# Two gated FFN input projections as seven products per pair of tiles, on two token blocks of 428

## Chip, cores and metric

The kernel runs on one core of one Trainium2 chip. The metric is the device time of one execution in microseconds: 2782.41 us is the median of three runs (2781.95 to 2783.56).

## The reference, cut to what matters

A two-layer encoder trunk works on 1024 prompt tokens and 64 sample tokens that share all weights. Each layer is a mixer with residual, then a gated FFN with residual:

```
def conv_ffn(h, st, w_in, conv_w, conv_b, w_out):
    gu = h @ w_in                              # (1088 x 1024) @ (1024 x 5632)
    g, u = gu[..., :D_FF], gu[..., D_FF:]      # D_FF = 2816
    g, new_st = causal_dwconv(g, conv_w, conv_b, st)     # width 3, along the tokens
    return (gelu(g) * u) @ w_out, new_st       # back to 1024
...
x = x + mixer(rmsnorm(x, norm_mix[l]))         # layer 0: SSD + short conv; layer 1: RG-LRU
x = x + conv_ffn(rmsnorm(x, norm_ffn[l]), ...)
```

All of it is float32, and a last RMSNorm gives the output.

## The kernel before

Activations lie channel by token: a tile has 128 channels on the partitions and T = 1092 columns (1024 prompt tokens, 4 of padding, 64 sample tokens). A projection to one output tile of 128 channels takes KT = 8 input tiles. For accuracy each float32 operand is held as a rounded high part and a low part (the rest), both in the type `float32r`, and a product is three: high by high, low weight by high, high weight by low. The 1092 columns go through TensorE in NB = 3 blocks of BL = 364, each into its own bank of a PSUM tile `pm` (two of these tiles, three banks each). So one output tile costs 8 x 3 x 3 = 72 matmuls of 364 columns (`product`, L160, called by `project`, L176).

Weights come by the SP queue in float32 (`weights`, L122): two halves of 512 columns, each loaded into `raw`, copied to the high part `wh` on ACT (L131), and the low part `wl` subtracted on DVE (L132). `prefetch` (L173) does so ahead of a named projection.

The FFN (`ffn`, L603) handles its 22 tiles of the hidden width one at a time in `make` (L608): project the gate tile, multiply by the row scale of the RMSNorm RS (L615, out of PSUM), convolve (`conv`, L230: first tap on ACT, L236, two more on DVE, L238; history columns by POOL, L228), gelu on ACT (L618), times RS (L619), project the up tile, multiply it in (L622), and split the result into high and low `ring` tiles (L186, L187). `chunks` (L288) collects two such tiles and flushes them (`chunk`, L257): for each of the 8 output tiles, 18 matmuls over the two hidden tiles, and a DVE addition into the residual tile XR[m] (L262), which stays in SBUF (`xr`). At the last flush `Next` (L266) makes each finished XR[m] ready for the next stage: scaled and split into `xg` (L192, L193), squared on ACT (L282), and the squares summed by accumulating DMAs on POOL's queue (L283); with a spill, XR[m] is also written to DRAM (L275). `rms` (L204) turns the sums into RS. `finish` (L735) does the last flush of layer 1 block by block.

The code gives an order, but the order on each engine is set when the program is built, by a planner with modelled durations: of the instructions that are ready at a time it takes the one that stands first in the code. Buffers of a tag (`wk` has 5, `ring` 8, `xr` 8, `xg` 16, `raw` 3, `wh` and `wl` 6 each) are handed out as they come free, and the instruction that first writes one waits for that. Heads of the SSD advance in steps between matmuls (`between`, `tick`, L151).

```
for (wh, wl), (xh, xl) in terms:
    for w, x in ((wh, xh), (wl, xh), (wh, xl)):
        for b in range(NB):
            TE.matmul(ps[:, b, 0:BL], w, x[:, b * BL:(b + 1) * BL], start=i == 0, stop=i == n - 1)
```

Of the kernel before, what the change touches and what calls it, by code (L numbers as in the profile page):

```python
# [22 lines left out]
BL = T // NB  # L23
NCH = L // P
# [29 lines left out]
def program(nc, tc, a, ctx):  # L54
# [11 lines left out]
    def slot(tag, bufs, dt=F, cols=T):  # L66
        n_of[tag] = n_of.get(tag, 0) + 1
        return sl.tile([P, cols], dt, tag=tag, bufs=bufs, name=f"{tag}{n_of[tag]}")

    def xg(dt=R):  # L70
        return slot("xg", 16, dt)

    def xr(dt=F, cols=T):
        return slot("xr", 8, dt, cols)
# [47 lines left out]
    def weights(src):  # L122

        out = []
        for i in range(2):
# [3 lines left out]
            l = wp.tile([P, 512], R, tag="wl", bufs=6, name=f"wl{n}")  # L129
            nc.sync.dma_start(raw, src[:, i * 512:(i + 1) * 512])  # L130
# [59 lines left out]
    def split_scaled(src, scale, make):  # L190
        h, l = make(R), make(R)
# [4 lines left out]
    def sum_square(ss, src, first, by=V):  # L196
        if first:
            S.activation(ss, src, AF.Square)
        else:
            sq = wk()  # L200
            S.activation(sq, src, AF.Square)
            by.tensor_add(ss, ss, sq)

    def rms(ss, width, more=None):  # L204

        v, r, out = wk(), wk(), ss
# [49 lines left out]

    def chunk(xs, ws, XR, done=None):  # L257

        for m in range(KT):
            ps = psum()  # L260
            product(ps, [(piece(w, m), x) for w, x in zip(ws, xs)])
            V.tensor_add(b3(XR[m]), b3(XR[m]), ps[:, :, 0:BL])  # L262
            if done:
                done(m)

    class Next:  # L266


        def __init__(self, XR, key, make=None, spill=None):
            self.XR, self.key, self.xs, self.spill = XR, key, [], spill  # L270

        def __call__(self, m):
            self.xs.append(split_scaled(self.XR[m], col(self.key, m), xg))
            if self.spill is not None:
                nc.gpsimd.dma_start(self.spill[m], self.XR[m])  # L275
            if m == 0:
                self.ss = [slot("ss", 2), slot("ss", 2)]
            if m < 2:
                S.activation(self.ss[m], self.XR[m], AF.Square)
            else:  # L280
                sq = wk()
                S.activation(sq, self.XR[m], AF.Square)  # L282
                nc.gpsimd.dma_start(self.ss[m % 2], sq, accum_op=OP.add)  # L283
# [4 lines left out]
    def chunks(n, produce, w_out, XR, done, after):  # L288

        tiles = {}  # L290

        def flush(i):
            ws = [weights(w_out[i]), weights(w_out[i + 1])]
            if i + 2 == n and after:
                prefetch(after)
            use = [tiles.pop(i), tiles.pop(i + 1)]
            if i + 2 == n and not after:
                done(use, ws)
            else:
                chunk(use, ws, XR, done if i + 2 == n else None)  # L300

        for i in range(n):
            tiles[i] = produce(i)
            if i % 2 == 0 and 2 <= i < n - 2:
                flush(i - 2)
        flush(n - 4)
        flush(n - 2)
# [4 lines left out]
    for k in range(KT):  # L312
# [3 lines left out]
        XGs.append(split_scaled(t, col("mix0", k), xg))  # L316
        if k == 0:

            raw_dt = wp.tile([P, 512], F, tag="raw", bufs=3, name="raw_dt")[:, 0:3 * H * KT].rearrange("p (k n) -> p k n", k=KT)
            w_dt = wp.tile([P, 512], R, tag="wh", bufs=6, name="w_dt")[:, 0:3 * H * KT].rearrange("p (k n) -> p k n", k=KT)  # L320
# [115 lines left out]
    def heads(i, xs, zz):  # L436
# [64 lines left out]
        Hn = small([P, P], "hn", 1)  # L501
# [83 lines left out]
    XR, RS2 = [], {}  # L585
    for m in range(KT):
        t = xr()
        nc.gpsimd.dma_start(t, a["x"][:, m])
        XR.append(t)

    def ab_tile(i):
# [9 lines left out]
        return split(y, ring)  # L601

    def ffn(layer, XGs, rs, XR, done, after):  # L603
        kind = f"ffn{layer}"

        state = {}

        def make(f):  # L608
            ps = project(("f_in", layer, 2 * f), XGs)
            if f == 0:  # L610
                prefetch(("f_in", layer, 1))
                state["rs"] = rs()
            RS = state["rs"]
            cb = conv_buffer()
            V.tensor_mul(b3(cb[:, PAD:]), ps, b3(RS))  # L615
            g = wk()
            conv(cb, kind, f, g)
            S.activation(g, g, AF.Gelu_apprx_tanh)  # L618
            V.tensor_mul(g, g, RS)  # L619
            ps = project(("f_in", layer, 2 * f + 1), XGs)  # L620
            hh = wk()
            V.tensor_mul(b3(hh), ps, b3(g))  # L622
            return split(hh, ring)

        chunks(FT, make, a["f_out"][layer], XR, done, after)

    nxt = Next(XR, "fn0")
    chunks(16, ab_tile, a["ab_out"], XR, nxt, ("f_in", 0, 0))
    x_d = scratch("x_d", [KT, P, T])
    last, nxt = nxt, Next(XR, "mix1", spill=x_d)  # L630
    ffn(0, last.xs, last.rs, XR, nxt, ("lru_in", 8))
# [89 lines left out]
    XR = []  # L721
    for m in range(KT):
        t = xr()
        nc.gpsimd.dma_start(t, x_d[m])
        XR.append(t)

    def c_tile(i):
        g = wk()
        nc.gpsimd.dma_start(g, hs_d[i])
        return split(g, ring)  # L730

    nxt = Next(XR, "fn1")
# [183 lines left out]
```

## Time and profile before

| | |
|---|---|
| median of three runs | 2782.41 us |
| profiled execution | 2783.79 us |
| its span, first to last instruction | 2782.0 us |
| mean granted TensorE clock | 0.996 of 2.4 GHz |
| busy: PE, DVE, ACT, POOL | 99%, 56%, 29%, 7% |
| instructions: PE, DVE, ACT, POOL | 16660, 1723, 1083, 521 |

PE is TensorE's matmuls, PEld its weight loads, which run beside them. DVE is VectorE, ACT ScalarE, POOL GpSimd, SP the queue that issues most loads. A group's row gives line, engine, operation, out<-in, shape and count, then busy time and the mean duration of one in ns. Matmuls overlap in the records: the time that one takes from the next is read from the starts in a timeline, not from its duration.

### The profile page before, as it was taken

What the parts mean: (1) busy time and instruction counts of PE and PEld (TensorE: products, weight loads), DVE (VectorE), ACT (ScalarE), POOL (GpSimd) and SP (SyncE); (2) the same over time, 40 slices, a digit from 0 to 9 for tenths busy, and PEclk for the clock granted to TensorE, in tenths of its full rate; (3) what the DMA queues carried; (4) which work ended last, traced back from release to release, by engine and by line L of the source; (5) the groups of instructions that cost most, each with busy time, mean ns of one, the idle gap of its engine ahead of it and who ended that gap; (6) DMA issues with size and microseconds to landing.
All of it is one profiled execution on the core that took longest, in us unless ns stands there. A gap on an engine that the chain in (4) does not pass through costs nothing.

```text
span 2782.0 us, 39199 instructions
## 1 busy us (share of the span) xinstructions
PE 2747.3 (99%) x16660; PEld 2716.6 (98%) x16660; DVE 1569.0 (56%) x1723; ACT 803.4 (29%) x1083; POOL 195.4 (7%) x521
## 2 busy tenths in 40 slices
PE   8999999999999999999999999999999999999998
PEld 8999999999999999999999989999999999999997
DVE  7655665568665444444444567786644444444446
ACT  7323322232142112211211245551421211212223
POOL 1101111110000000000000010120000000000003
PEclk9999999999999999999999999999999999999999
DMA  3222322243231111111111141151311111111111
GB/s 132 78 82 82 100 98 82 83 132 135 71 94 40 44 46 46 46 43 46 42 46 46 63 131 58 55 196 57 89 44 46 45 44 46 42 46 44 41 47 68
DMA packets 85695, 193.08 MB, mean 69 GB/s; under 512 B 10096, under 2 KB 12704, under 8 KB 85520
## 3 DMA queue, kind: packets, MB, share of 16 engines
q1 hardware_dynamic: 67248, 123.40, 13.3%
q0 software_dynamic: 17984, 66.76, 8.0%
q8 instruction: 131, 2.15, 0.3%
q10 hardware_dynamic: 288, 0.42, 0.0%
q14 instruction: 44, 0.36, 0.0%
HBM read 156.81 MB, written 23.66 MB: 65 GB/s over the span
## 4 chain that ended last, share of the span: by engine, by line
PE 93%; DVE 2%; DMA 2%; issue 1%; ACT 1%; POOL 0%; DVEq 0%; POOLq 0%; ACTq 0%
PE pm L167 90%; DMA ss<-wk 2%; PE pa L514 1%; PE pa L487 1%; PE pm L750 1%; DVE xg L779 0%; PE pa L525 0%; PE pm L334 0%; DVE xr L262 0%; DMA hs_d<-ring 0%; PE pa L210 0%; PE pa L212 0%; PE pa L472 0%; DVE xg L193 0%; DMA par<-par 0%
## 5 line engine op out<-in xcount | busy, mean ns | idle before, releaser
L167 PE MATMUL pm<-xg,wh 128*128 128x364 f32 x7104 | 1409.1, 331 | 0.0
L167 PEld LDWEIGHTS pm<-xg,wh 128*128 128x128 f32 x7104 | 1205.2, 189 | 6.6 <-issue 3.1
L167 PE MATMUL pm<-xg,wl 128*128 128x364 f32 x3552 | 783.4, 329 | 0.0
L131 ACT ACTIVATE wh<-raw 128x512 fp32r<-128x512 f32 x440 | 274.4, 628 | 1472.6 <-PE pm L167 1250.8
L167 PE MATMUL pm<-ring,wh 128*128 128x364 f32 x3360 | 656.8, 329 | 5.7 <-DVE xr L262 1.9
L167 PEld LDWEIGHTS pm<-xg,wl 128*128 128x128 f32 x3552 | 620.6, 188 | 0.5
L167 PEld LDWEIGHTS pm<-ring,wh 128*128 128x128 f32 x3360 | 570.6, 188 | 8.3 <-DVE xr L262 2.5
L262 DVE TENSOR_TENSOR xr<-xr,pm 128x1092 f32<-128x1092 f32 x264 | 340.8, 1291 | 211.8 <-PE pm L167 205.8
L132 DVE TENSOR_TENSOR wl<-raw,wh 128x512 fp32r<-128x512 f32 x440 | 300.5, 685 | 252.5 <-ACT wh L131 252.2
L167 PE MATMUL pm<-ring,wl 128*128 128x364 f32 x1680 | 372.0, 330 | 0.0
L167 PEld LDWEIGHTS pm<-ring,wl 128*128 128x128 f32 x1680 | 293.5, 188 | 0.1
L238 DVE SCALAR_TENSOR_TENSOR wk<-wk,par,wk 128x1092 f32<-128x1092 f32 x104 | 140.9, 1355 | 64.1 <-ACT wk L236 62.6
L615 DVE TENSOR_TENSOR wk<-pm,ss 128x1092 f32<-128x1092 f32 x44 | 57.0, 1296 | 192.9 <-PE pm L167 192.7
L228 POOL COPY wk<-par 128x2 f32<-128x2 f32 (+1 forms) x72 | 40.5, 563 | 1723.7 <-DVE wk L615 1426.5
L622 DVE TENSOR_TENSOR wk<-pm,wk 128x1092 f32<-128x1092 f32 x44 | 57.0, 1295 | 119.6 <-PE pm L167 119.6
L187 DVE TENSOR_TENSOR ring<-wk,ring 128x1092 fp32r<-128x1092 f32 x68 | 88.0, 1296 | 38.6 <-ACT ring L186 32.8
L186 ACT ACTIVATE ring<-wk 128x1092 fp32r<-128x1092 f32 x68 | 75.7, 1116 | 101.5 <-PE pm L167 67.5
L236 ACT ACTIVATE wk<-wk,par 128x1092 f32<-128x1092 f32 x52 | 67.7, 1302 | 67.6 <-POOL wk L228 67.6
L619 DVE TENSOR_TENSOR wk<-wk,ss 128x1092 f32<-128x1092 f32 x44 | 57.0, 1297 | 52.1 <-ACT wk L618 52.1
L618 ACT ACTIVATE wk<-wk 128x1092 f32<-128x1092 f32 x44 | 49.2, 1118 | 120.8 <-DVE wk L238 120.8
L238 DVE SCALAR_TENSOR_TENSOR xr<-wk,par,xr 128x1092 f32<-128x1092 f32 x36 | 48.8, 1354 | 15.4 <-ACT xr L236 14.8
L193 DVE SCALAR_TENSOR_TENSOR xg<-xr,par,xg 128x1092 fp32r<-128x1092 f32 x32 | 43.3, 1354 | 10.7 <-ACT xg L192 10.4
(243 smaller groups left out, 1308.9 us busy)
## 6 DMA issues: line engine op xcount, KB each, us to landing
raw<-f_in SPq DMA_DIRECT2D x176, 256.0 KB, 2.5
raw<-ab_in SPq DMA_DIRECT2D x88, 256.0 KB, 2.6
raw<-f_out SPq DMA_DIRECT2D x88, 256.0 KB, 2.5
ss<-wk POOLq DMA_DIRECT2D x18, 546.0 KB, 7.0
ring<-at_d POOLq DMA_DIRECT2D x16, 546.0 KB, 6.1
raw<-ab_out SPq DMA_DIRECT2D x32, 256.0 KB, 2.6
raw<-lru_in SPq DMA_DIRECT2D x32, 256.0 KB, 2.5
xr<-x SPq DMA_DIRECT2D x8, 546.0 KB, 7.9
```

The lines of the kernel that those rows point to most:

```text
L131: S.activation(h, raw, AF.Copy)
L132: V.tensor_sub(l, raw, h.bitcast(F))
L167: TE.matmul(ps[:, b, 0:BL], w, x[:, b * BL:(b + 1) * BL], start=i == 0, stop=i == n - 1)
L186: S.activation(h, src, AF.Copy)
L187: V.tensor_sub(l, src, h.bitcast(F))
L236: S.activation(out, cb[:, at:at + T], AF.Identity, bias=col(kind + "_b", i), scale=col(kind + "_w", i * w))
L238: V.scalar_tensor_tensor(out, cb[:, at + k:at + k + T], col(kind + "_w", i * w + k), out, op0=OP.mult, op1=OP.add)
L262: V.tensor_add(b3(XR[m]), b3(XR[m]), ps[:, :, 0:BL])
L615: V.tensor_mul(b3(cb[:, PAD:]), ps, b3(RS))
L618: S.activation(g, g, AF.Gelu_apprx_tanh)
L619: V.tensor_mul(g, g, RS)
L622: V.tensor_mul(b3(hh), ps, b3(g))
```

## The change

In both FFNs, tiles are taken in pairs: two neighbouring gate tiles (or two up tiles) by the two halves of the 1024 inputs (HK = 4 tiles each) by two token blocks of SB = 428 columns are a two-by-two block product, computed with seven block products in place of eight (Winograd's form of Strassen's scheme). The sums of input blocks t1 to t4 are made once per layer (`Pairs`, a `Next`), the sums of weights for each pair of tiles (`Ready`), both ahead of the split into high and low parts. The last RB = 236 columns are projected plainly. `seven` issues the products in an order, copies partial sums that are used twice out of PSUM (`held`, on ACT) and goes on accumulating onto them; `Ready.step` is called four times in between for the next pair. All 22 pairs of a layer (11 gate, 11 up, in turn) come first; the gated rows go to DRAM (`h_d`) and are read back tile by tile for the output projection, which is done after them; the residual is written to DRAM and read back into `ring` tiles. Output weights are prepared for half the output tiles at a time, and the last chunks ahead of each FFN take four tiles at once. `wh`/`wl` have 4 buffers, `raw` 2 of twice the size; tags are x0, x1 (8 each), x2 (8 of 1284 columns) in place of xg and xr.

```diff
+SB = 428
+RB = T - 2 * SB
...
-            raw = wp.tile([P, 512], F, tag="raw", bufs=3, name=f"raw{n}")
-            h = wp.tile([P, 512], R, tag="wh", bufs=6, name=f"wh{n}")
+            raw = raws[:, i * 512:(i + 1) * 512]
+            h = wp.tile([P, 512], R, tag="wh", bufs=4, name=f"wh{n}")
...
+    PLACE = {"b21": (0, B[0]), "b22": (0, B[1]), "k1": (0, B[2]), "t3": (1, B[0]), "t4": (1, B[1]), "k0": (1, B[2]),
+             "t1": (2, B[0]), "t2": (2, B[1]), "b11": (2, slice(2 * SB, 3 * SB))}
+    class Pairs(Next):
+        order = [m for k in range(HK) for m in (k, k + HK)]
+        def operands(self, m):
+            if m < HK:
+                return
...
+            h, l = zip(*[(x(R), x(R)) for x in (x0, x1, lambda dt: x2(dt, 3 * SB))])
...
+            scaled(0, slice(0, T), r1, w1, slice(0, T))
+            S.activation(t4, r0[:, B[0]], AF.Copy, scale=w0)
+            V.scalar_tensor_tensor(t1, r0[:, B[1]], w0, t4, op0=OP.mult, op1=OP.subtract)
+            V.scalar_tensor_tensor(t2, r1[:, B[1]], w1, t1, op0=OP.mult, op1=OP.subtract)
+            V.tensor_sub(t3, t2, t4)
+            V.scalar_tensor_tensor(t4, r1[:, B[0]], w1, t2, op0=OP.mult, op1=OP.subtract)
+            scaled(1, B[2], r0, w0, B[2])
+            scaled(2, slice(2 * SB, 3 * SB), r0, w0, B[0])
+            plain(2, ta)
+            plain(1, tb)
+            self.xs.append((h, l))
+            if len(self.xs) > 2:
+                self.first.step()
...
+    class Ready:
...
+                raw = wp.tile([P, 1024], F, tag="raw", bufs=2, name=f"raw{n}")
+                nc.sync.dma_start(raw, a[key[0]][key[1:]])
...
+            def place(name):
+                self.w[name] = ring(R, 1024), ring(R, 1024)
+            def ready(name, raw):
+                h, l = self.w[name]
+                S.activation(h, raw, AF.Copy)
+                V.tensor_sub(l, raw, h.bitcast(F))
+            place("a2")
+            ready("a2", r1)
+            V.tensor_add(r1[:, hi], r1[:, lo], r1[:, hi])
+            V.tensor_sub(r1[:, lo], r0[:, lo], r1[:, lo])
+            yield
+            place("a1")
+            ready("a1", r0)
+            V.tensor_sub(r0[:, lo], r1[:, hi], r0[:, lo])
+            V.tensor_sub(r0[:, hi], r0[:, hi], r0[:, lo])
+            yield
+            place("s24")
+            place("s31")
+            last = [("s24", r0), ("s31", r1)]
+            if self.swap:
+                last.reverse()
+            ready(*last[0])
+            yield
+            ready(*last[1])
+            yield
+    def seven(ws, X, put, plain, end, nxt, mode="mid", rs=None):
+        ta, tb = psum(), psum()
+        pw, v1, v0 = ta[:, 0, 0:SB], ta[:, 1, 0:RB], ta[:, 2, 0:RB]
+        px, py, pz = tb[:, 0, 0:SB], tb[:, 1, 0:SB], tb[:, 2, 0:SB]
+        def mul(ps, w, half, name, start=True, ks=range(HK)):
...
+                for i, (wx, x) in enumerate(((wh, xh), (wl, xh), (wh, xl))):
+                    TE.matmul(ps, wx, x, start=start and k == 0 and i == 0, stop=k == HK - 1 and i == 2, skip_group_check=True)
+        def held(ps):
+            n = n_of["cp"] = n_of.get("cp", 0) + 1
+            t = wp.tile([P, 512], F, tag="wh", bufs=4, name=f"cp{n}")[:, 0:SB]
+            S.activation(t, ps, AF.Copy)
+            return t
+        def V1():
+            mul(v1, "a2", 0, "k0")
+            mul(v1, "a2", 1, "k1", False)
+        def V0():
+            mul(v0, "a1", 0, "k0")
+            mul(v0, "a1", 1, "k1", False)
+        def W():
+            mul(pw, "a2", 1, "t4")
+        def Z1():
+            mul(pz, "s31", 1, "t1")
+        def Z2():
+            mul(pz, "s24", 1, "b22", False)
+        def X1():
+            mul(px, "a1", 0, "b11")
+        def X2():
+            mul(px, "s24", 0, "t2", False)
+        def X3():
+            mul(px, "s31", 0, "t3", False)
+        def Y():
+            mul(py, "a1", 1, "b21")
+        if mode == "mid":
+            W()
+            V1()
+            w = held(pw)
+            Z1()
+            plain(1, v1)
+            step()
+            X1()
+            p5 = held(pz)
+            V0()
+            p1 = held(px)
+            X2()
+            Y()
+            plain(0, v0)
+            u2 = held(px)
+            step()
+            put(0, 0, py, p1)
+            Z2()
+        elif mode == "first":
+            ws.step()
+            Y()
+            mul(v1, "a2", 1, "k1")
+            mul(v0, "a1", 1, "k1")
+            ws.step()
+            for k in range(HK):
+                mul(px, "a1", 0, "b11", True, [k])
+                mul(pz, "s31", 1, "t1", True, [k])
+                mul(pw, "a2", 1, "t4", True, [k])
+                mul(v1, "a2", 0, "k0", False, [k])
+                mul(v0, "a1", 0, "k0", False, [k])
...
+            rs()
+            plain(1, v1)
+            step()
+            X2()
...
+        else:
+            Z1()
+            X1()
+            p5 = held(pz)
+            W()
+            p1 = held(px)
+            X2()
+            w = held(pw)
+            V1()
+            u2 = held(px)
+            V0()
...
+        step()
+        X3()
+        put(0, 1, pz, u2)
+        put(1, 0, px, w)
+        put(1, 1, px, p5)
+        step()
+        end(0)
+        end(1)
...
-    def ffn(layer, XGs, rs, XR, done, after):
+    def ffn(layer, X, done, after):
...
+            def put(m, b, ps, t):
+                V.tensor_add(cbs[m][:, PAD + b * SB:PAD + (b + 1) * SB], ps, t)
+            def end(m):                      # gate pair
...
+                V.tensor_mul(cb[:, two], cb[:, two], RS[:, two])
+                g = wk()
+                conv(cbs[m], kind, 2 * p + m, g)
+                S.activation(g, g, AF.Gelu_apprx_tanh)
+                V.tensor_mul(g, g, RS)
...
+            def end(m):                      # up pair
+                V.tensor_mul(us[m][:, two], us[m][:, two], gs[m][:, two])
+                nc.gpsimd.dma_start(h_d[2 * p + m], us[m])
...
+            def plain(m, ps):
+                V.tensor_mul(us[m][:, B[2]], ps, gs[m][:, B[2]])
...
+        XR = residual(lambda m: X.spill[m])
+        def h_tile(f):
+            h = slot("ss", 2) if f == 1 else wk()
+            nc.gpsimd.dma_start(h, h_d[f])
+            return split(h, x2)
+        chunks([2] * (FT // 2), h_tile, a["f_out"][layer], XR, done, after)
...
+    def chunks(sizes, produce, w_out, XR, done, after, order=range(KT)):
...
+            ws = out_weights(w_out, i, size, 0)
+            for p, m in enumerate(order):
+                if p == KT // 2:
+                    ws = out_weights(w_out, i, size, 1)
+                    if last:
+                        after()
+                ps = psum()
+                at = slice(p % 4 * P, (p % 4 + 1) * P)
+                product(ps, [((h[:, at], l[:, at]), x) for (h, l), x in zip(ws, tiles[i:i + size])])
+                V.tensor_add(b3(XR[m]), b3(XR[m]), ps[:, :, 0:BL])
+                if last:
+                    done(m)
+            i += size
...
+    def residual(src):
+        out = []
+        for m in Pairs.order:
+            t = ring()
+            nc.gpsimd.dma_start(t, src(m))
...
+        return split(y, x1 if i < 14 else x2)
...
+    nxt = Pairs(XR, "fn0", scratch("xa_d", [KT, P, T]))
+    chunks([2] * 6 + [4], ab_tile, a["ab_out"], XR, nxt, first_weights(nxt, 0), Pairs.order)
```

## Rows read from the trace of the kernel before

**Rows 1.** The page: busy time by engine, then the chain that ended last by engine and by line.
```profile
PE 2747.3 (99%) x16660; PEld 2716.6 (98%) x16660; DVE 1569.0 (56%) x1723; ACT 803.4 (29%) x1083; POOL 195.4 (7%) x521
...
PE 93%; DVE 2%; DMA 2%; issue 1%; ACT 1%; POOL 0%; DVEq 0%; POOLq 0%; ACTq 0%
PE pm L167 90%; DMA ss<-wk 2%; PE pa L514 1%; PE pa L487 1%; PE pm L750 1%; DVE xg L779 0%; PE pa L525 0%; PE pm L334 0%; DVE xr L262 0%; DMA hs_d<-ring 0%; PE pa L210 0%; PE pa L212 0%; PE pa L472 0%; DVE xg L193 0%; DMA par<-par 0%
```

**Rows 2.** The chain in order of time: start us, us, what.
```profile
819.91 7.34 DMA ss<-wk
...
830.94 763.65 PE pm L167 x4589
```

**Rows 3.** Windows of layer 0's FFN and after it: engines' busy us, clock, DMA share.
```profile
core 0: us, PE busy (x) PEld busy (x) DVE busy (x) ACT busy (x) POOL busy (x), PEclk, DMA share, GB/s
1000.00:1048.00 48.00, 48.00 (x291) 48.00 (x290) 24.66 (x24) 11.92 (x14) 1.64 (x8) 1.00 0.14 43
1048.00:1096.00 48.00, 48.00 (x290) 48.00 (x289) 19.54 (x20) 8.49 (x11) 1.11 (x5) 1.00 0.14 46
...
1612.00:1636.00 24.00, 18.18 (x79) 14.83 (x78) 8.43 (x22) 9.94 (x15) 2.51 (x5) 0.79 0.69 190
```

**Rows 4.** Timeline of PE in steady work: start us, us, instructions.
```profile
645.21 1.16 PE L167 MATMUL pm<-ring,wh 128*128 128x364 f32 x6
646.21 0.67 PE L167 MATMUL pm<-ring,wl 128*128 128x364 f32 x3
```

**Rows 5.** Timeline of PE where the shape of weights or columns differs.
```profile
24.23 0.66 PE L334 MATMUL pm<-xg,w_dt 128*48 128x364 f32 x3
24.72 0.50 PE L167 MATMUL pm<-xg,wh 128*128 128x364 f32 x2
...
81.94 0.67 PE L383 MATMUL pa<-idm,ring 16*128 16x16 f32 x8
82.46 0.18 PE L384 MATMUL pa<-idm,ring 16*64 16x16 f32 x1
```

**Rows 6.** Groups of DVE by line and shape: busy us, mean ns | idle before.
```profile
L132 DVE TENSOR_TENSOR wl<-raw,wh 128x512 fp32r<-128x512 f32 x440 | 300.5, 685 | 252.5 <-ACT wh L131 252.2
L238 DVE SCALAR_TENSOR_TENSOR wk<-wk,par,wk 128x1092 f32<-128x1092 f32 x104 | 140.9, 1355 | 64.1 <-ACT wk L236 62.6
L619 DVE TENSOR_TENSOR wk<-wk,ss 128x1092 f32<-128x1092 f32 x44 | 57.0, 1297 | 52.1 <-ACT wk L618 52.1
L462 DVE TENSOR_TENSOR ring<-ring,xr 128x1024 f32<-128x1024 f32 x16 | 19.6, 1222 | 3.5 <-ACT ring L460 3.4
L753 DVE TENSOR_TENSOR xr<-xr,pm 128x364 f32<-128x364 f32 x24 | 11.5, 527 | 8.6 <-PE pm L750 8.6
```

**Rows 7.** Groups of ACT by line and shape.
```profile
L236 ACT ACTIVATE wk<-wk,par 128x1092 f32<-128x1092 f32 x52 | 67.7, 1302 | 67.6 <-POOL wk L228 67.6
L618 ACT ACTIVATE wk<-wk 128x1092 f32<-128x1092 f32 x44 | 49.2, 1118 | 120.8 <-DVE wk L238 120.8
L460 ACT ACTIVATE ring<-ring 128x1024 f32<-128x1024 f32 x16 | 16.7, 1045 | 0.0
L754 ACT ACTIVATE xg<-xr 128x364 f32<-128x364 f32 x24 | 11.2, 506 | 23.2 <-DVE xr L753 23.2
```

**Rows 8.** Timeline of ACT through one gate tile.
```profile
1016.60 0.63 ACT L131 ACTIVATE wh<-raw 128x512 fp32r<-128x512 f32 x1 [3.59 <-PE pm L167]
1022.59 0.64 ACT L131 ACTIVATE wh<-raw 128x512 fp32r<-128x512 f32 x1 [5.36 <-PE pm L167]
1024.52 1.30 ACT L236 ACTIVATE wk<-wk,par 128x1092 f32<-128x1092 f32 x1 [1.29 <-POOL wk L228]
1028.64 1.12 ACT L618 ACTIVATE wk<-wk 128x1092 f32<-128x1092 f32 x1 [2.82 <-DVE wk L238]
```

**Rows 9.** DMA issues of the page and the queue view: count, KB each, median us to landing.
```profile
raw<-f_in SPq DMA_DIRECT2D x176, 256.0 KB, 2.5
ysc_d<-wk POOLq DMA_DIRECT2D x8, 546.0 KB, 3.5
x_d<-xr POOLq DMA_DIRECT2D x8, 546.0 KB, 7.0
xr<-x_d POOLq DMA_DIRECT2D x8, 546.0 KB, 5.1
```

**Rows 10.** Timeline of DVE at the opening of layer 0's FFN.
```profile
815.10 1.29 DVE L262 TENSOR_TENSOR xr<-xr,pm 128x1092 f32<-128x1092 f32 x1
...
833.07 0.54 DVE L222 SCALAR_TENSOR_TENSOR ss<-ss,wk 128x364 f32<-128x364 f32 x1
```

More of the change, by code (lines that the diff above doesn't have):

```diff
@@ L282, in __call__ @@
                 S.activation(sq, self.XR[m], AF.Square)
-                nc.gpsimd.dma_start(self.ss[m % 2], sq, accum_op=OP.add)
+                nc.gpsimd.dma_start(self.ss[self.n % 2], sq, accum_op=OP.add)
+            self.n += 1
         def rs(self):
             return rms(self.ss[0], D, self.ss[1])
[L288 to L307, printed above, removed]
+    HK = KT // 2
@@ new lines, in chunks, with until @@
+    def chunks(sizes, produce, w_out, XR, done, after, order=range(KT)):
+        n, tiles = sum(sizes), []
+        order = list(order)
+        def until(i):
+            while len(tiles) < min(i, n):
+                tiles.append(produce(len(tiles)))
+        i = 0
+        for size in sizes:
+            last = i + size == n
+            until(i + size + 1)
+            if last and isinstance(done, Finish):
+                ws = [out_weights(w_out, i, size, half) for half in range(2)]
+                done(tiles[i:], list(zip(*ws)))
+                return
+            ws = out_weights(w_out, i, size, 0)
[11 more added lines that the diff above has]
+            i += size
@@ L600, in ab_tile @@
             RS2[0] = rms(ssz[0], D)
-        return split(y, ring)
-    def ffn(layer, XGs, rs, XR, done, after):
+        return split(y, x1 if i < 14 else x2)
+    def ffn(layer, X, done, after):
         kind = f"ffn{layer}"
+        h_d = scratch(f"h_d{layer}", [FT, P, T])
+        two = slice(0, 2 * SB)
         state = {}
[L608 to L625, printed above, removed]
@@ new lines, in up, with put, plain @@
+        def up(p, gs):
+            us = [wk(), wk()]
+            def put(m, b, ps, t):
+                V.tensor_add(us[m][:, B[b]], ps, t)
+            def end(m):
+                V.tensor_mul(us[m][:, two], us[m][:, two], gs[m][:, two])
+                nc.gpsimd.dma_start(h_d[2 * p + m], us[m])
+            def plain(m, ps):
+                V.tensor_mul(us[m][:, B[2]], ps, gs[m][:, B[2]])
+            return put, plain, end
+        groups = [(p, u) for p in range(FT // 2) for u in range(2)]
@@ new lines, in ready @@
+        def ready(g):
+            p, u = g
+            return Ready(*[("f_in", layer, 2 * (2 * p + m) + u) for m in range(2)])
+        ws = X.first
+        gs = None
+        for n, (p, u) in enumerate(groups):
+            nw = ready(groups[n + 1]) if n + 1 < len(groups) else None
+            if u == 0:
+                todo, gs = gate(p)
+            else:
+                todo = up(p, gs)
+            seven(ws, X, *todo, nw, "first" if n == 0 else "last" if nw is None else "mid", rs)
+            ws = nw
@@ L720, in program @@
         xb = nx
[L721 to L725, printed above, removed]
+    XR = residual(lambda m: x_d[m])
     def c_tile(i):
```

176 lines of the change are left out of this document (130 added, 46 removed).

## The prediction

> **What bounds the kernel now.** I read the page first. PE is busy for 99% of the span, DVE for 56%, ACT for 29%, and the chain that ended last is PE for 93%, of which 90% is the one line that issues the large products [rows 1]. Busy PE is no proof by itself, since the matmul records overlap, so I looked at the chain in order of time: through layer 0's FFN it is one unbroken piece of 763.65 us with 4589 matmuls, 166.4 ns each [rows 2]. The reader is to see there that nothing else ever ends last inside an FFN. The windows agree: in two stretches of 48 us PE is full at clock 1.00, while DVE does 24.66 and 19.54 us and ACT 11.92 and 8.49 [rows 3]. So in this stage fewer columns through TensorE are worth their full time, as long as the work that the change gives to DVE and ACT still fits beside it.
>
> **The spacing of matmuls.** Six matmuls start within 646.21 - 645.21 = 1.00 us [rows 4], so one 364-column matmul takes 166.7 ns: 364 / 2.4 = 151.7 ns of columns and 15.0 ns more. For 428 columns I take 428 / 2.4 + 15 = 193.3 ns, for 236 columns 98.3 + 15 = 113.3. If the excess grew with the columns it would be 196.0 and 108.1, and the group below comes to 21.65 us in place of 21.68, so that choice is immaterial. What is not shown is a narrow matmul of this kind. Its lower bound is the bare columns, 98.3 ns. The upper bound is 166.7: a weight load that sets the spacing would do so whatever the columns. Two rows decide between them. Three matmuls with weights of 48 columns start within 24.72 - 24.23 = 0.49 us, 163 ns each: a load less than half as wide buys nothing. And eight with 16 columns behind loads of 128 weight columns start within 82.46 - 81.94 = 0.52 us, 65 ns each [rows 5]. So a load and its matmul pass in 65 ns when the columns are few, and 113.3 stands, near the lower end.
>
> The Trainium skill ("TensorE: Matmul & The Clock Gate", section "Back-to-back issue gap") gives N / 2.4 + 2.5 ns at full clock. The row's 166.7 against its 154.2 for 364 columns disagrees. An estimate by that page would be 22.20 us before and 20.03 after for a pair of tiles, some 7 us less gained over the kernel than by the rows.
>
> **What TensorE saves.** A pair of tiles costs 2 x 72 = 144 matmuls of 364 now: 144 x 166.7 = 24.00 us. After: seven products of 4 x 3 = 12 matmuls of 428, and 2 x 8 x 3 = 48 of 236: 84 x 193.3 + 48 x 113.3 = 16.24 + 5.44 = 21.68 us. There are 22 pairs in each layer, 44 in all: 44 x 2.32 = 102 us off the path. The bounds: 21.07 us (narrow at 98.3), 129 us; 24.24 us (narrow at 166.7), minus 11 us. The output projections keep their matmuls.
>
> **Whether DVE and ACT still fit.** DVE's rows lie on a line: 685 ns for 512 columns, 1222 for 1024, 527 out of PSUM for 364 [rows 6], so 0.147 us + 1.05 ns a column: 0.60 us for 428, 1.05 for 856, 0.40 for 236. `Ready` makes four low parts of 1024 and four sums of 512: 4 x 1.222 + 4 x 0.685 = 7.6 us. The four `put` cost 2.4, the two `plain` 0.8. Each gate tile adds 1.05 + 2 x 1.355 + 1.297 = 5.06 us in `end`, each up tile 1.05. So DVE has 20.9 us for a gate pair, 12.9 for an up pair, 33.8 in 43.4 us of PE, 78%. ACT: four copies of 1.045, three `held` of about 0.57 (from 0.506 for 364) and for gate pairs 2 x (1.302 + 1.118): 10.7 and 5.9 us [rows 7]. Both fit. Neither engine hides less than PE gives.
>
> The order inside a pair decides whether they fit at the right moment. I walk a gate pair followed by an up pair, from the end of the gate's X3, with PE at W 2.3, V1 5.0, Z1 7.4, X1 9.7, V0 12.4, X2 14.7, Y 17.0, Z2 19.4, X3 21.7 us.
> - Z1 writes the PSUM tile that the last two `put` read, and uses s31, whose ring buffers are the ones X3 has just released. ACT copies s31 by 1.3, DVE does the two `put` by 1.5 and its low part by 2.7; Z1 starts at 5.0. Margin 2.3 us.
> - The gate's `end` work, 10.1 us, then runs on DVE with two hops to ACT and one to POOL, from 2.7 to about 14.5. The next weights need their raw tile loaded again after s31's low part: 512 KB, about 5 us if twice the 2.5 of 256 KB [rows 9]; behind that load on SP wait only further weights. a2 is ready by 16, needed at 21.7; a1's buffers are released by Y at 17.0, its parts and sums end near 20.6, needed at 28; s24 follows Z2 and ends at 23 to 25, needed at 34.
> - `held` of px lies between X1 (9.7) and X2 (12.4): 0.2 + 0.57 us, or 1.9 if a gelu is in front of it. Queued behind it on ACT are the other `held` and the copies of the next weights, which have slack.
>
> In the up window DVE is then at 20.4 of 21.7 us, counting two muls and the rest that spill into it, in the gate window at some 13. So no stall follows on paper. I take 0.25 us a pair for the moments at which an op of 1.3 us stands in front of an urgent one: 11 us in all. Bounds: 0, and 2 us for each pair.
>
> It rests on the planner interleaving. It does so now: the copies for the up tile's weights, at 1016.60 and 1022.59, stand behind the gelu in the code and run ahead of it (1028.64) [rows 8], while PE has no gap [rows 3].
>
> **The edges.**
> - Opening of each FFN. The last output product's XR[7] needs an addition (1.29 us), a scaled split, three more sums and two more splits on DVE: about 7.7 us until the last pair of operands stands, and the x2 buffers of the last input tile come free only with that product. PE has v1, v0 and Y for three of four k (3.8 us), then the products of three k (7.2 us). That covers it, unless s31 (2.3 us, written after those in the code) comes last and holds the second part. I take 4 us each, bounds 0 and 8: 8 us. RS: 18.5 us now from the last addition (815.10) to the last step of the row scale (833.60) [rows 10], 7.34 of it one accumulating DMA [rows 2]; the first group's 21.7 us covers it. The new spill adds 8 writes of 7.0 us [rows 9] to that queue, but products now come every 6 us, not every 3.
> - After layer 0's FFN PE does 18.18 us of work in 24 at clock 0.79 [rows 3], waiting for the same sums. Nothing in that is changed; I cost it at nothing.
> - From the last up pair to the output products: h tiles are split into x2 buffers released by the first four products of the "last" order, 12 us ahead. The residual's loads take 5.1 us [rows 9] and go into ring buffers that a2 and a1 leave; an addition is needed every 3 us. I take 1 us each, bounds 0 and 5: 2 us.
> - `h_d`: 44 writes of 3.5 us (like `ysc_d`) and as many reads on a POOL queue that is 7% busy, in a stage with a DMA share of 0.14 [rows 1, 3, 9]. Behind a write on POOL stand the history columns of the next gate, 20 us later. No cost; if writes took 10 us the `wk` buffers would still be free before the next gate's g.
> - In the mixers fewer weight buffers (two keys in place of three) and the residual of layer 0 waiting for SSD's ring buffers: PE's products of 12 us cover a load of 5. I take 3 us, bounds 0 and 12.
>
> **Sum.** -102 + 11 + 8 + 2 + 3 = -78 us. The profiled execution took 2783.8 us, 2782.0 of span and 1.8 around it, 1.4 above the median of the runs shown, so against that 2705.8, and against the median 2782.4 - 78 = 2704.
>
> **Rivals.**
> - DVE or ACT late in the up windows. For it: 94% of that window by the sum above, with POOL and ACT hops in the chain. Against: 60% in the window after it. At the upper bound of 2 us on each of 22 gate-to-up changes it costs 44 us, and with both openings at 8 us, 8 more, less the 6 already in the sum for those pairs: about 2750.
> - Narrow matmuls cost what wide ones do. The place is V1 and V0, 48 of 132 matmuls; at 166.7 ns a pair takes 24.24 us, and with the 24 us of other losses the time is 2782 + 11 + 24 = 2817. It decides from (24.0 - 16.2) / 48 = 162 ns on, or 150 with the losses. For it: weight loads are busy for 98% [rows 1]. Against it: the 65 ns of rows 5.
>  The Trainium skill ("Perfetto Trace Analysis", section "Identifying the Most-Contended Engine") counts busy weight loads as the measure of how near TensorE is to its limit; that would give this rival's 2817, and rows 5 speak against reading it so here.
> - The queues run a gate's `end` in code order, tile after tile: two chains of about 8.5 us ahead of the next `held`. PE would stand before X2 from 12.4 to about 22 us, 22 times: +211 us, 2915. It is slower from 3.5 us a change on. Against it: rows 8.
>
> **How the numbers follow.** Forecast (range of its own 2678 to 2728) 0.66; late DVE or ACT 0.20; narrow at the price of wide 0.05; code order, or waits above 3.5 us a change from any such chain, 0.05; a gain above 104 us 0.04. From 2674 to 2765 holds 8 in 10 and a little more. What a measurement can tell here is 0.2%, 5.6 us. Faster: 0.66 + 0.04 + 0.17 of the 0.20 = 0.87; within 0.2%: the other 0.03; slower: 0.05 + 0.05 = 0.10.
>
> **What would show it.** The matmuls fall from 16660 to 16132. Starts of wide ones should lie 193 to 196 ns apart, of narrow ones 108 to 114; at 150 or more the second rival holds. Windows of 43.4 us in the FFN should hold one gate and one up pair, with PE full and DVE 34 us busy. A gap ahead of each X2 with ACT's `held` as releaser means the third rival; gaps ahead of Z1 with `put` or s31, the first. PE gaps above 8 us at either opening would make my edges wrong.

## The result, and the profile after

The changed kernel takes 2990.64 us (median of four runs, 2984.39 to 2991.01) against 2782.18 us for the kernel before on the same chip: a ratio of 1.074, 95% interval [1.073, 1.076]. It is slower by 208 us where 78 us of gain were forecast. The profiled execution took 2990.91 us.

The page after, beside [rows 1]: PE has fallen from 99% to 92% of the span although it has 528 matmuls fewer, DVE and ACT have risen, and two of the forty slices show a granted clock below 9 tenths of full speed. L408 issues the products of the pairs; its row ends with the idle time before it.

```profile
span 2989.1 us, 38889 instructions
...
PE 2759.9 (92%) x16132; PEld 2653.2 (89%) x16132; DVE 1872.8 (63%) x2203; ACT 964.1 (32%) x1292; POOL 262.2 (9%) x641
...
PEclk9999999999999899899999999999999999999999
...
L408 PE MATMUL pm<-x,ring 128*128 128x428 f32 (+1 forms) x5808 | 1064.6, 345 | 181.3 <-ACT cp L413 93.5
```

The waits of PE in the kernel after (waiting line and what it waited for: us in total, times, longest us) name three releasers for most of it: ACT's copies out of PSUM (`held`, L413), and the multiplications out of PSUM of a gate pair (L895) and of an up pair (L910), both `plain`, on DVE. None of the three has a term of its own in the forecast's sum; the third rival prices the first.

```profile
PE pm L408 <- ACT cp L413: 93.5, 18, 5.2
PE pm L408 <- DVE wk L895: 40.9, 22, 4.2
PE pm L408 <- DVE wk L910: 21.5, 20, 5.1
PE pm L408 <- DVE wk L882: 9.2, 22, 2.7
```

Windows of one gate group, the up group behind it, and three stretches inside the up group (columns as in [rows 3]: busy us of PE, PEld, DVE, ACT and POOL, the granted clock, DMA's share):

```profile
1167.76:1192.14 24.38, 22.49 (x134) 21.15 (x132) 12.16 (x16) 5.91 (x8) 2.91 (x9) 1.00 0.27 91
1192.14:1223.53 31.39, 25.20 (x134) 23.24 (x132) 19.55 (x22) 10.64 (x12) 0.10 (x1) 0.89 0.11 34
1202.00:1208.00 6.00, 0.81 (x5) 0.45 (x4) 6.00 (x6) 3.98 (x6) 0.10 (x1) 0.91 0.00 0
1208.00:1213.00 5.00, 4.37 (x17) 3.76 (x18) 2.43 (x4) 0.00 (x0) 0.00 (x0) 0.50 0.00 0
1213.00:1218.00 5.00, 5.00 (x31) 4.88 (x30) 0.40 (x1) 0.00 (x0) 0.00 (x0) 0.93 0.00 0
```

A group should take 21.68 us. The gate group takes 24.38 and the up group 31.39, and no other engine is full there: DVE is busy for 19.55 us of the 31.39. PE stands almost empty from 1202 to 1208. In the 5 us from 1208 the granted clock is 0.50, the 1.2 GHz level: 17 matmuls start there, beside a gap of 0.63 us, where the next 5 us hold 31.

PE's timeline (start us, us, instructions, idle before and its releaser) shows where, first in the gate group, then in the up group:

```profile
1173.50 4.75 PE L408 MATMUL pm<-x,ring 128*128 128x428 f32 x23 [0.19 <-DVE ring L374]
1179.75 10.14 PE L408 MATMUL pm<-x,ring 128*128 128x236 f32 x62 [1.50 <-DVE wk L895]
...
1197.87 4.75 PE L408 MATMUL pm<-x,ring 128*128 128x428 f32 x23 [0.19 <-DVE ring L374]
1207.81 1.44 PE L408 MATMUL pm<-x,ring 128*128 128x428 f32 x3 [5.18 <-ACT cp L413]
1209.88 11.41 PE L408 MATMUL pm<-x,ring 128*128 128x236 f32 x59 [0.63 <-DVE wk L910]
```

All three gaps stand at the same place, after X1: the next products are V0 (236 columns) and X2 (three of whose matmuls the planner has put ahead of V0). ACT and DVE in the same stretches:

```profile
1177.07 1.06 ACT L373 ACTIVATE ring<-raw 128x1024 fp32r<-128x1024 f32 x1 [5.51 <-DMA raw<-f_in]
...
1201.44 1.07 ACT L373 ACTIVATE ring<-raw 128x1024 fp32r<-128x1024 f32 x1
1204.13 1.11 ACT L890 ACTIVATE wk<-wk 128x1092 f32<-128x1092 f32 x1 [1.62 <-DVE wk L250]
1205.40 1.11 ACT L890 ACTIVATE wk<-wk 128x1092 f32<-128x1092 f32 x1 [0.15 <-DVE wk L250]
1206.42 1.34 ACT L413 ACTIVATE cp<-pm 128x428 f32<-128x428 f32 x3
```

```profile
1178.16 1.23 DVE L374 TENSOR_TENSOR ring<-raw,ring 128x1024 fp32r<-128x1024 f32 x1 [2.79 <-ACT ring L373]
1179.30 0.40 DVE L895 TENSOR_TENSOR wk<-pm,ss 128x236 f32<-128x236 f32 x1
...
1200.21 5.16 DVE L250 SCALAR_TENSOR_TENSOR wk<-wk,par,wk 128x1092 f32<-128x1092 f32 x4 [0.47 <-ACT wk L248]
1205.28 1.22 DVE L374 TENSOR_TENSOR ring<-raw,ring 128x1024 fp32r<-128x1024 f32 x1
1206.41 2.50 DVE L891 TENSOR_TENSOR wk<-wk,ss 128x1092 f32<-128x1092 f32 x2
1208.83 0.69 DVE L378 TENSOR_TENSOR raw<-raw 128x512 f32<-128x512 f32 x1
1209.43 0.40 DVE L910 TENSOR_TENSOR wk<-pm,wk 128x236 f32<-128x236 f32 x1
```

- **Up group, X2.** X1 ends about 1202.5. The copy of its partial sum, which X2 needs, takes half a us and ACT is idle from 1202.5 to 1204.1. But in ACT's queue the three copies stand behind both gelus, and the second gelu waits for the second convolution on DVE, done at 1205.4. So the copies run at 1206.42. The Trainium skill ("Perfetto Trace Analysis", section "Tensor Engine Instruction (MATMUL, LD_WEIGHTS)") says in passing that ACT, DVE and GpSimd run strictly first in, first out; the 1.62 us that ACT idles with ready copies behind the gelu agree.
- **Up group, V0.** V0 writes one bank of the PSUM tile `ta`; `plain(1)` reads V1's result from another bank of the same tile, and V0 waits for that read. In an up pair `plain(1)` multiplies by the finished gate rows, so it stands behind both multiplications L891 and ran at 1209.43. That tile has a second late reader: W's result lies in it too, and its copy is one of the three behind the gelus. Here it ended before `plain(1)`; the first experiment brings it out.
- **Gate group, V0.** The same tile, another queue: `plain(1)` stands on DVE behind a2's low part, and its high part had waited on ACT for a 512 KB load (5.51 us idle).
- **Smaller ones.** Z1 and Z2 each lose about 0.35 us in most groups (to s31's low part, and to `put(0, 0)`, which reads Y out of the tile that Z2 writes). The first group of each layer takes 35.3 and 36.8 us, the last gate group 29.6 and 29.7 (Z1 of the last order waits up to 2.7 us for the `put`, L882).

I added up the distances between the starts of all matmuls of the pairs. What lies above 195 ns (428 columns) or 113 ns (236) by more than 0.3 us, the gaps, is 216.7 us in 170 places; what lies above by 0.05 to 0.3 us is 72.8 us over 633 matmuls. Of these 72.8 us, 59.2 (514 matmuls) stand in stretches with the granted clock at 0.50, where matmuls of 236 columns start 213 ns apart and those of 428 columns 358; the other 13.6 us, at full clock, are small waits. Together 289.5 us, where the forecast had 21 (11 for the pairs, 8 and 2 at their ends).

### The profile page after: what moved, and what is told of

Same layout as the page of the kernel before. It is cut to its first block, busy times and chain, and to the rows that moved or that the text cites. A ratio compares the mean times of both kernels' runs of the same rounds, so it can differ in the third digit from the quotient of the medians.

```text
span 2989.1 us, 38889 instructions
## 1 busy us (share of the span) xinstructions
PE 2759.9 (92%) x16132; PEld 2653.2 (89%) x16132; DVE 1872.8 (63%) x2203; ACT 964.1 (32%) x1292; POOL 262.2 (9%) x641
## 5 line engine op out<-in xcount | busy, mean ns | idle before, releaser
L408 PE MATMUL pm<-x,ring 128*128 128x428 f32 (+1 forms) x5808 | 1064.6, 345 | 181.3 <-ACT cp L413 93.5
L408 PEld LDWEIGHTS pm<-x,ring 128*128 128x128 f32 x5808 | 990.0, 203 | 255.0 <-ACT cp L413 111.3
L179 PE MATMUL pm<-x,wh 128*128 128x364 f32 x6048 | 1204.6, 331 | 10.2 <-DVE ring L556 7.5
L179 PEld LDWEIGHTS pm<-x,wh 128*128 128x128 f32 x6048 | 1027.4, 188 | 20.2 <-DVE ring L556 8.8
L179 PE MATMUL pm<-x,wl 128*128 128x364 f32 x3024 | 669.5, 330 | 0.7 <-DVE wl L526 0.6
L179 PEld LDWEIGHTS pm<-x,wl 128*128 128x128 f32 x3024 | 527.4, 189 | 2.0 <-DVE wl L526 1.6
L374 DVE TENSOR_TENSOR ring<-raw,ring 128x1024 fp32r<-128x1024 f32 x176 | 215.0, 1223 | 379.4 <-ACT ring L373 373.3
L556 DVE TENSOR_TENSOR ring<-ring,pm 128x1092 f32<-128x1092 f32 x248 | 319.8, 1290 | 192.1 <-PE pm L179 187.8
L143 ACT ACTIVATE wh<-raw 128x512 fp32r<-128x512 f32 x128 | 79.0, 626 | 335.1 <-PE pm L179 334.7
L144 DVE TENSOR_TENSOR wl<-raw,wh 128x512 fp32r<-128x512 f32 x128 | 86.7, 683 | 39.9 <-ACT wh L143 39.8
L413 ACT ACTIVATE cp<-pm 128x428 f32<-128x428 f32 x176 | 82.2, 517 | 21.4 <-PE pm L408 21.4
L910 DVE TENSOR_TENSOR wk<-pm,wk 128x236 f32<-128x236 f32 x44 | 17.5, 402 | 99.3 <-PE pm L408 99.3
```

Source lines behind the costliest of these rows:

```text
L408: TE.matmul(ps, wx, x, start=start and k == 0 and i == 0, stop=k == HK - 1 and i == 2, skip_group_check=True)
L413: S.activation(t, ps, AF.Copy)
```

## The experiments

The theory (A in most expectations) was: two orders are wrong, V0 behind `plain(1)` through the shared tile, and the copies behind the gelus. The rivals were that one of them hides the other or is the whole cause, and later that the tile of X, Y and Z has a wait of its own. Each time is a median (of two to five runs), with its ratio to the kernel before and the 95% interval; the last column has the medians of the gate and up groups in a layer, without its first group and its last two.

| kernel | us | ratio | median gate, up group, us |
|---|---|---|---|
| changed | 2990.6 | 1.074 [1.073, 1.076] | 24.5, 31.4 |
| plain_after_v0 | 2910.6 | 1.047 [1.044, 1.049] | 23.3, 28.9 |
| gelu_after_held | 2917.1 | 1.049 [1.047, 1.051] | 24.5, 28.7 |
| both_moved | 2806.7 | 1.009 [1.007, 1.011] | 23.3, 23.7 |
| v0_own_tile | 2852.8 | 1.026 [1.024, 1.028] | 22.6, 26.8 |
| tiles_only | 2810.0 | 1.010 [1.008, 1.012] | 21.7, 26.1 |
| moves_and_y_tile | 2755.2 | 0.990 [0.989, 0.992] | 21.7, 21.7 |
| own_tiles_both | 2715.6 | 0.976 [0.975, 0.978] | 21.7, 21.7 |
| reordered | 2759.3 | 0.992 [0.991, 0.994] | 21.8, 22.6 |

**plain_after_v0: `plain(1)`, the multiplication out of PSUM, behind V0.**

```diff
             Z1()
-            plain(1, v1)
             step()
             X1()
             p5 = held(pz)
             V0()
+            plain(1, v1)
             p1 = held(px)
```

> In the middle groups the product of the second plain tile, plain(1, v1), is written behind V0 in the code in place of ahead of it. Theory A (order): V0 waits for plain(1) because both use one PSUM tile, and plain(1) of an up pair needs the gate pair's finished rows; on top of it the copies held sit behind both gelus on ACT. This edit takes the first wait away and leaves the second: gate pairs fall from 24.5 to about 22.5 us, up pairs from 31.8 to about 28, in all about 2885 us (2860 to 2915). Theory B (DVE has too much to do in the up windows, my first rival): the order of the code changes nothing, 2975 to 3000 us.

It gained 80 us and left the copies as the wait; that is 26 us less than theory A's value, near the slow end of its range. V0's wait for `plain(1)` is gone, but V0 is not free. In PE's and ACT's timelines of an up group the first matmuls after the gap have 236 columns, so they are V0's, and they start as the first of the three copies ends (1179.17 + 0.51 us). In the code's order that is the copy of W, which lies in V0's tile: its second reader, still behind both gelus. All 40 waits for copies in this run (93.9 us) stand before V0; X2 follows it without a gap.

```profile
1179.73 5.84 PE L408 MATMUL pm<-x,ring 128*128 128x236 f32 x25 [4.36 <-ACT cp L413]
...
1178.15 1.11 ACT L890 ACTIVATE wk<-wk 128x1092 f32<-128x1092 f32 x1 [0.15 <-DVE wk L250]
1179.17 1.34 ACT L413 ACTIVATE cp<-pm 128x428 f32<-128x428 f32 x3
```

**gelu_after_held: the gelus and their multiplications behind the third copy.** The gate's `end` hands them over, and the next pair issues them after that copy; `plain(1)` stays ahead of V0.

```diff
+    held_last, rest_of_gate = [None], []
...
-            S.activation(t, ps, AF.Copy)
+            held_last[0] = S.activation(t, ps, AF.Copy).ins
...
+        def late():
+            with tc.issue_after(held_last[0]):
+                while rest_of_gate:
+                    rest_of_gate.pop(0)()
...
-            plain(1, v1)
             step()
             X1()
             p5 = held(pz)
+            p1 = held(px)
+            late()
+            plain(1, v1)
             V0()
-            p1 = held(px)
             X2()
...
-                S.activation(g, g, AF.Gelu_apprx_tanh)
-                V.tensor_mul(g, g, RS)
                 gs.append(g)
+                def gelu():
+                    S.activation(g, g, AF.Gelu_apprx_tanh)
+                    V.tensor_mul(g, g, RS)
+                rest_of_gate.append(gelu)
```

> The gelu and the last multiplication of a gate pair are written behind the third copy held of the next pair and kept behind it on ACT's queue; plain(1) stays ahead of V0. Theory A: the copies come on time, but V0 still waits for plain(1), so gate pairs stay at 24.5 us and up pairs come to 29 to 31: 2945 to 2985 us. If ACT's queue alone were the cause: up pairs 24.5, about 2845 us. Theory B: 2975 to 3000 us.

2917.1 us is below theory A's range and above the figure for ACT's queue alone: the copies are most of the way out (93.5 us down to 27.5), and V0's wait for the up pair's `plain(1)`, L923 here, has taken their place (PE's waits):

```profile
PE pm L410 <- DVE wk L923: 43.7, 19, 2.8
PE pm L410 <- DVE wk L908: 40.3, 22, 4.2
PE pm L410 <- ACT cp L415: 27.5, 20, 3.0
```

**both_moved: the two together** (`late()` and `plain(1)` both behind V0).

> Both moves together: V0 ahead of plain(1), and the gelus behind the copies held. Theory A: neither wait is left, gate and up pairs at about 22.7 us, 2990 - 20 x (9.1 + 1.8) = about 2770 us (2750 to 2800), near the time of the kernel before; the rest of the expected gain is still missing in the first and the last groups of each layer. Theory B: DVE's 34 us of a gate and an up pair do not shrink, up pairs stay above 28 us and the time above 2880 us.

184 us gained, but the time is 7 us above the range given: the two orders were the larger part, not all. PE's timeline of an up group has gaps of 0.36 us (V0, again until the first copy ends) and, later, 0.58 us (W of the next group, until both `plain` have read the tile that it writes):

```profile
1058.32 7.66 PE L410 MATMUL pm<-x,ring 128*128 128x236 f32 x48 [0.36 <-ACT cp L415]
1066.55 5.73 PE L410 MATMUL pm<-x,ring 128*128 128x428 f32 x29 [0.58 <-DVE wk L923]
```

**v0_own_tile: the changed kernel's order, V0 in a PSUM tile of its own.**

```diff
-        pw, v1, v0 = ta[:, 0, 0:SB], ta[:, 1, 0:RB], ta[:, 2, 0:RB]
+        pw, v1, v0 = ta[:, 0, 0:SB], ta[:, 1, 0:RB], aux().rearrange("p a b -> p (a b)")[:, 0:RB]
```

> v0 lies in a PSUM tile of its own (one bank of the small pool) in place of the third bank of the tile of v1; the order of the code is that of the changed kernel. If V0 waits for plain(1) only because they share a PSUM tile (theory A): as with plain(1) moved behind V0, about 2885 us (2860 to 2915). If V0 waits for something else on DVE (a weight's low part, an input's): no change, 2975 to 3000 us.

It gained 138 us without moving an instruction in the code, 7 us more than the range allowed and 58 more than moving `plain(1)`: a tile of its own frees V0 from both readers, `plain(1)` and the copy of W. V0's waits are gone from gate and up groups; in the up groups 2.5 us before X2 remain (`ACT cp L413: 51.5, 21, 2.8` in PE's waits). This is the direct evidence for the shared tile.

**own_tiles_both: both moves, and V0 and Y in tiles of their own.** In a layer's first group the tiles stay shared and `put(0, 0)` goes behind X3 instead.

```diff
+        if mode != "first":
+            v0, py = (aux().rearrange("p a b -> p (a b)")[:, 0:n] for n in (RB, SB))
...
             u2 = held(px)
-            put(0, 0, py, p1)
             step()
             Z2()
...
         X3()
+        if mode == "first":
+            put(0, 0, py, p1)
```

> Both moves (V0 ahead of plain(1), gelus behind the copies held), and besides v0 and py in PSUM tiles of their own outside the first group, and in the first group put(0, 0) written behind X3. Theory A (waits by shared PSUM tiles and by the order on ACT's queue are the whole loss in the middle groups): gate pairs 22.6 us as in the run with v0 in its own tile, up pairs the same, the first group of each layer 4 us shorter; in all 2806.7 - 20 x (0.6 + 1.1) - 8 = about 2765 us (2745 to 2780), faster than the kernel before. Theory B (DVE's work sets the up windows): up pairs stay above 23.5 us, 2795 to 2810 us.

2715.6 us, 2.4% faster than the kernel before, about 50 us better than expected and below the range: in the middle groups the gaps that both_moved had left went with the shared tiles. Some 12 of the 91 us stand in the two first groups (35.7 and 35.9 us there, 30.0 and 29.8 here), where only `put(0, 0)` was moved. Windows of a gate and an up group, then PE's timeline through them: no row of the pairs has idle time before it, DVE fills 19.74 of 21.72 us, and the clock stays at full.

```profile
1042.47:1064.15 21.68, 21.68 (x133) 21.15 (x132) 12.26 (x16) 6.05 (x9) 2.90 (x9) 1.00 0.30 101
1064.15:1085.87 21.72, 21.72 (x133) 21.14 (x132) 19.74 (x22) 10.49 (x13) 0.10 (x1) 1.00 0.16 49
```

```profile
1041.69 10.61 PE L412 MATMUL pm<-x,ring 128*128 128x428 f32 x64
1052.14 2.84 PE L412 MATMUL pa<-x,ring 128*128 128x236 f32 x24
1054.83 2.48 PE L412 MATMUL pm<-x,ring 128*128 128x428 f32 x12
1057.14 2.50 PE L412 MATMUL pa<-x,ring 128*128 128x428 f32 x12
1059.48 14.53 PE L412 MATMUL pm<-x,ring 128*128 128x428 f32 x84
```

Counted as above, 11.9 us of gaps and 3.6 us of smaller waits are left, none of it at a granted clock of 0.50. That is 274 us less than in the changed kernel; the medians differ by 275.

**tiles_only: own tiles without the moves.**

> The changed kernel in its own order of code (the last product's write of the small half still ahead of V0, the two gelus still ahead of the copies), with one edit: V0 and Y get PSUM tiles of their own, outside a layer's first group. Theory A (the shared tiles and the copies behind the gelus are two causes, each with its own price): the gate groups lose every gap and come to 21.7 us, the up groups keep the 2.65 us before X2 that V0's own tile alone left, which is waited for from ScalarE's copies, 24.5 to 25.2 us. Against the 2852.8 us of V0's own tile alone that takes away two gaps of 0.35 us from each of 42 groups, 29 us: 2824 us (2805 to 2840). Theory B (the order of code no longer matters once the tiles are apart, since the planner then places the copies early): no gap in the up groups either, 2716 to 2745 us.

2810.0 us, theory A: the gate groups are clean, and the up groups keep one wait for the copies, though they are 0.9 us longer than its range for them. ACT's timeline shows the copies behind both gelus and a weights' copy; PE goes on at 1057.27. The windows show what the wait costs beyond itself: 26.1 - 21.7 = 4.4 us for 2.60 us of idle. Most of the rest are the ten matmuls behind it, nearly all some 356 ns apart in place of 195: 1.6 us, at a granted clock of 0.50.

```profile
1052.64 2.38 ACT L892 ACTIVATE wk<-wk 128x1092 f32<-128x1092 f32 x2 [2.77 <-DVE wk L250]
1054.93 0.51 ACT L415 ACTIVATE cp<-pm 128x428 f32<-128x428 f32 x1
1055.34 1.05 ACT L373 ACTIVATE ring<-raw 128x1024 fp32r<-128x1024 f32 x1
1056.29 0.93 ACT L415 ACTIVATE cp<-pm 128x428 f32<-128x428 f32 x2
```

```profile
1055.50:1058.50 3.00, 1.23 (x3) 1.17 (x4) 2.88 (x4) 1.72 (x3) 0.00 (x0) 0.80 0.00 0
1058.50:1061.00 2.50, 2.50 (x9) 2.34 (x8) 1.21 (x3) 0.00 (x0) 0.00 (x0) 0.56 0.00 0
1061.00:1066.00 5.00, 5.00 (x28) 4.85 (x27) 1.88 (x3) 1.59 (x2) 0.00 (x0) 1.00 0.00 0
```

So moves and tiles overlap: each alone is worth 184 and 181 us, the second on top of the first 91 and 94. Either frees V0 for the most part; only the moves take the gelus from in front of X2's copy, and only the tiles free Z2.

**moves_and_y_tile: both moves, only Y's tile apart.** The edit is that of tiles_only for `py` alone, on both_moved.

> The kernel with both moves (last product's write behind V0, gelus behind the copies; 2806.7 us), with one edit: Y gets a PSUM tile of its own outside the first group, V0 stays in the tile that it shares with W and V1. Theory A (each shared tile costs its own gaps): the 0.35 us before Z2 goes from some 42 groups, 15 us, and the 0.4 to 1.9 us that stand at V0's own matmuls and before it stay: 2785 us (2770 to 2798). Theory B (the gaps in both_moved come from the tile that X, Y and Z share, whose late reader sets the whole order): all of the 91 us between this kernel and the one with all tiles apart goes, 2716 to 2745 us.

Between the two theories, 2755.2 us: Y's tile brings most groups to 21.7 us, as B has it, and 31 us of what is left are something else: PE waits 15.7 us in each layer where it goes over from pairs to output products. POOL's timeline shows why: the first read of `h_d` (L951) stands in POOL's queue behind the residual's loads (L860), and these wait for PE to release ring buffers.

```profile
1307.28 1.06 POOL L860 DMA_DIRECT2D ring<-xa_d  x2 [22.80 <-PE pm L412]
...
1317.10 0.54 POOL L922 DMA_DIRECT2D h_d<-wk  x1 [2.28 <-DVE wk L921]
...
1319.12 1.58 POOL L951 DMA_DIRECT2D wk<-h_d  x3
```

In own_tiles_both the planner put one such read in between, and PE waits 1.7 us there:

```profile
1297.00 1.06 POOL L861 DMA_DIRECT2D ring<-xa_d  x2 [23.25 <-PE pm L412]
1298.05 0.53 POOL L952 DMA_DIRECT2D wk<-h_d  x1
```

With own_tiles_both's handover it would stand at about 2755 - 2 x 14 = 2727 us, an estimate inside B's range. So V0's shared tile matters little once `plain(1)` is behind V0 and the copies run ahead of the gelus; the 12 us that are left include the first groups, where own_tiles_both has `put(0, 0)` moved as well.

**reordered: own_tiles_both with the products in the order W, V1, V0, Z1, X1, Y, X2, Z2, X3.**

```diff
             W()
             V1()
             w = held(pw)
-            Z1()
+            V0()
             step()
+            Z1()
             X1()
             p5 = held(pz)
-            V0()
+            Y()
             p1 = held(px)
             late()
             plain(1, v1)
             X2()
-            Y()
             plain(0, v0)
```

> As the run with its own tiles, and the products in another order: W, V1, V0, Z1, X1, Y, X2, Z2, X3 in the middle groups, so that 2.7 us more stand ahead of Z1, which waits for the low part of s31; W and V1 first in the last group as well. Theory A: the gap of 0.36 us ahead of Z1 in each pair and the 2.9 us ahead of the last group's Z1 go, 40 x 0.4 + 2 x 4 = 24 us less than the run with its own tiles: about 2741 us (2725 to 2760). If X2 now comes too early for its copy (only Y, 2.3 us, lies between): a gap of 0.2 to 1 us ahead of each X2, 2750 to 2790 us.

44 us worse than own_tiles_both, at the slow end of theory A's range and inside that of the fallback. In the up groups (22.6 us) Y no longer stands between X2 and Z2: Z2 waits 0.62 us for the copy of X2's sum, which reads another bank of the tile that Z2 writes (13.9 us in 21 waits for copies in all). That is some 18 us in all, in the fallback's sense but one product later than it names. The larger part, 27 us, was in neither theory: the handover to the output products has the same long wait as above, here on PE. So the total in the fallback's range is luck.

```profile
1310.88 4.84 PE L412 MATMUL pm<-x,ring 128*128 128x428 f32 x24
1331.14 1.28 PE L179 MATMUL pm<-x,wh 128*128 128x364 f32 x3 [15.42 <-ACT x L198]
```

## Why the prediction was wrong, point by point

- **Matmuls and their spacing: right.** 16132 matmuls. Starts lie 195 ns apart for 428 columns (median of 3558) and 113 for 236 (1978), where 193.3 to 196.0 and 113.3 were worked out from [rows 4, 5]. A pair without stalls takes 21.68 to 21.72 us in own_tiles_both, so the 102 us were there to be had. The second rival, narrow at the price of wide, is out. One bound of that sum was misworked, without effect: 16.24 + 48 x 0.0983 is 20.96 us, not 21.07. And the rule that the prediction takes from the Trainium skill ("TensorE: Matmul & The Clock Gate", section "Back-to-back issue gap") is given there for a matmul on its own, not for a stream of loads and matmuls like this one.
- **Work on DVE and ACT: right in sum.** 19.55 and 12.16 us in the up and gate windows, where the walk had 20.4 and some 13. In own_tiles_both DVE works for 91% of the up window and PE loses nothing, so the first rival, as DVE short of time, is out as well. Its sign, a gap ahead of Z1 with s31 as releaser, was there at 0.36 us a group (0.19 idle); it goes in own_tiles_both with DVE's work unchanged.
- **The step that failed: the walk, "So no stall follows on paper", and its term "0.25 us a pair ... 11 us in all".** It measured 290 us with the ends of the layers: 217 in gaps, 59 in matmuls at the lower clock, 14 in small waits. Two omissions made it so. First, the walk gave `held` "0.2 + 0.57 us, or 1.9 if a gelu is in front of it": it charged the gelu's own time, and not what the gelu waits for. Two gelus stood in front, and the second waited for DVE's convolution: 5.2 us. Second, V0 was not walked as waiting for anything. The tile that it shares with V1 was in the code (`ta`), and `plain(1)` of an up pair reads `gs`, the last link of the gate's chain, which the walk itself had ending near 14.5 us while V0 was to start at 9.7. The copy of W, in the same tile, is on ACT behind the gelus: with `plain(1)` out of the way V0 waited 4.36 us for it.
- **"It rests on the planner interleaving."** [Rows 8] showed weights' copies running 6 and 12 us ahead of a gelu that stands before them in the code. Here the copy could have run 1.6 us ahead of the first gelu and 2.9 ahead of the second, and the planner kept the order of the code. That a lead of 6 us is used does not show that one of 2 us is; what its modelled times were here was not looked into.
- **The third rival came nearest.** Its sign, a gap ahead of X2 with ACT's `held` as releaser, is the largest wait after, and its price of 9.6 us a change is what an up group lost (31.39 - 21.68 = 9.7 us). But the composition differs. By the starts of the up group's matmuls 5.3 us are the gap for the copies, 1.0 that for `plain(1)`, 0.7 those before Z1 and Z2, and 2.3 the matmuls in the stretch at the lower clock. The agreement of 9.6 and 9.7 is luck. DVE interleaved the two chains; the code order that hurt was ACT's. It had a chance of 0.05, since [rows 8] was taken for all of ACT's copies.
- **A price that no step had.** What a stall does to the clock stands in no term of the sum. It is a fifth of the loss (59 of 290 us).
- **The ends of the layers.** First groups 35.3 and 36.8 us: 28.7 us above two clean ones, where 8 were taken; 16.4 remain in own_tiles_both. The order there was wrong too: the next group's W waits 3.67 us for the first group's `plain`. `h_d` at "no cost" holds in the changed kernel (writes 4.2 us, reads 5.0), but the queue that it shares with the residual's loads cost some 14 us a layer in two of the experiments.
- **The forecast for the algorithm itself** was nearly met by own_tiles_both: 2715.6 against 2704, in part because two errors cancel. The openings cost 8 us more than taken, but the pairs between openings and ends cost 1.5 us where 11 were taken. Of the 78 us the profiled run has 70.5 (spans 2711.5 and 2782.0): by the starts of the same matmuls the FFNs gave 78.2 us where 81 were forecast, and the mixers lost 7.7 where 3 were.

## What to carry to other kernels

When a walk puts a small urgent op on a queue, price what stands in front of it by when that work's inputs come, not by its duration, and check the order of code for exactly that pair of ops. List for every matmul group who last reads the PSUM tile that it writes, bank by bank or not, and what that reader itself waits for; a tile of its own was worth 138 us here without moving a line, and moving away one of its two late readers only 80. A saving of 2.3 us a pair is lost to a single stall of its size, and a stall of several us cost more than itself here.

## What the runs showed of the hardware that was not expected

- After PE had idled 5.18 us, the granted clock was 0.50, the 1.2 GHz level, from 1208 to 1213. In tiles_only it was 0.56 for 2.5 us soon after 2.60 us of idle. After 1.50 us in the changed kernel's gate group the window stayed at 1.00. Over the pairs of the changed kernel a stretch at 0.50 followed all 20 waits above 5 us and none of the 17 of 1.4 to 1.7 us; of the 20 waits of 2.5 to 2.8 us in v0_own_tile 15 were followed by one and 5 were not.
- The granted mean over the whole run (0.963 changed, 0.995 own_tiles_both) hides this: the page's tenths show only two slices below 9, while 514 matmuls of the pairs ran well above their full-clock spacing at 0.50.
